# Nearest-neighbour upsampling on one core: loads in four DMAs with 32 KiB descriptors, and one broadcast copy per engine and store

## The chip, the cores and the metric

The kernel runs on one core of one Trainium2 chip. In the profiles DVE is the core's VectorE, ACT its ScalarE and SP its SyncE. The metric is the device time of one execution in microseconds; lower is better. Times quoted are medians of several executions.

## The reference

```python
x = np.random.randn(16, 64, 64, 64).astype(np.float32)      # scale_factor = 2
result = np.zeros((16, 64, 128, 128), dtype=np.float32)
for i in range(128):
    for j in range(128):
        result[:, :, i, j] = x[:, :, i // 2, j // 2]
```

Each input row of 64 floats becomes two identical output rows of 128 floats, each input element twice in a row. 16.78 MB are read and 67.11 MB are written. There is no arithmetic.

## The kernel before

The input is seen as 65536 rows of 64 floats. A tile has 128 partitions with 32 rows each: 8 KiB in, 32 KiB out, per partition. All DMAs are issued by the SyncE engine (SP in the profile) on its one queue: nine loads first (two of 1 MiB, then seven of 2 MiB), then sixteen stores of 4 MiB.

```python
K = 32                                   # input rows per partition and tile
rows = P * K                             # 4096;  16 tiles
J = 2                                    # tiles per load
... # group = 8: the whole input fits in SBUF, so one pass
k_dve = (K + 1) // 2                     # 16 rows for DVE, 16 for ACT
xpool: bufs=group;   upool: bufs=2
for ti in range(ti0, ti0 + group):       # all loads
    xt = xpool.tile([P, J, K, W], fdt, name="xt")
    ... # the first load as two DMAs of 1 MiB, the others:
    src = src.rearrange("(j p k) w -> p j (k w)", j=J, p=P)
    nc.sync.dma_start(out=xt[:, :, :, :], in_=src)
for t in range(...):                     # expand and store, tile by tile
    u2 = upool.tile([P, K, s, W, s], fdt, name="u2")
    for ei, (lo, hi) in enumerate(((0, k_dve), (k_dve, K))):
        src_ap = xt[:, j, lo:hi, :]
        for hd in range(s):
            for wd in range(s):          # four strided copies per engine
                dst = u2[:, lo:hi, hd, :, wd]
                ... # nc.vector.tensor_copy (ei == 0) or nc.scalar.copy
    nc.sync.dma_start(out=of[r0 : r0 + rows, :], in_=u2[:, :, :, :, :])
```

## Time and profile before

The kernel took 200.79 us (200.72 to 201.0, three runs). The profiled execution has a span of 199.2 us.

The next fence is the profile page of the kernel before. Part 1 gives the busy time of each engine and its share of the span. The row "DMA" is the mean busy share of the 16 DMA engines in 40 equal slices of the span, in tenths, so that 9 means full; below it stand the GB/s moved. The queue lines give packets, MB and the share of 16 engines' time. The lines with a source line give one group of instructions: output and input shape, count, then busy us and mean ns of one, then the idle time before them and what ended it.

```profile
DVE 40.0 (20%) x64; ACT 68.0 (34%) x65; POOL 0.2 (0%) x4
...
DMA  6999999999999999999999999999999999999995
...
q1 hardware_dynamic: 4496, 83.89, 98.5%
q14 instruction: 3, 0.02, 0.0%
...
DMA 69%; ACT 18%; SPq 3%; ACTq 1%; issue 0%
...
L88 ACT COPY u<-xt 128x1024 f32<-128x1024 f32 x64 | 66.7, 1136 | 114.6 <-DMA out_dram<-u 111.0
L86 DVE COPY u<-xt 128x1024 f32<-128x1024 f32 x64 | 40.0, 690 | 141.7 <-DMA out_dram<-u 136.1
```

The DMA engines are full from the second slice to the last but one. No compute engine is near full.

The share of 18% for ACT in the chain of waits needs the timeline to be read. This is two rounds of the steady state, kernel before (start us, duration us, engine, instruction; in brackets the idle time before and its releaser):

```profile
62.25 4.17 ACT L88 COPY u<-xt 128x1024 f32<-128x1024 f32 x4 [5.43 <-DMA out_dram<-u]
62.27 2.50 DVE L86 COPY u<-xt 128x1024 f32<-128x1024 f32 x4 [7.08 <-DMA out_dram<-u]
...
71.96 4.18 ACT L88 COPY u<-xt 128x1024 f32<-128x1024 f32 x4 [5.55 <-DMA out_dram<-u]
```

A store lands about every 9.7 us and frees one of two buffers. ACT refills it in 4.17 us, while the other buffer's store is on the DMA engines. The chain alternates between ACT and a store, because each is released by the other, but the DMA row stays at 9: the 4.17 us cost nothing as long as they stay below 9.7.

The trace also has a record of every DMA packet. Times in the rest of this document that are "after the first packet" count from the start of the first data packet, about 1.7 us after the start of the span. In the kernel before:

| packets | number | duration | per DMA engine |
|---|---|---|---|
| loads, 8 KiB | 2048 | median 311 ns, the first 1.1 us | 40.58 us |
| stores, 32 KiB | 2048 | 1213 ns, hardly any spread | 155.34 us |

Together 195.9 us out of the span's 199.2 us are packet time on every engine. There is no more than about 3 us that is not transfer. (The records do not name the engine of a packet; "per engine" is the sum over all packets divided by 16.)

### The profile page before, as it was taken

Reading aid. Unit: us, or ns where it says so; the run is one execution under the profiler, and the core shown is the slowest. Engines: PE = TensorE matmul, PEld = TensorE weight load, DVE = VectorE, ACT = ScalarE, POOL = GpSimd, SP = SyncE. Lnnn points to the kernel's source line nnn. Section 1 sums busy time; section 2 is a strip of 40 time slices with the busy share of each in tenths; the row PEclk is TensorE's granted clock in tenths of the full one; section 3 lists DMA queues with packets and bytes.
Section 4 is the critical chain, followed back from the end, with each engine's and each line's share of the span. In section 5 each row is a group of like instructions: output and inputs, shape, how many; then the busy total and the mean of one; then the engine's idle time right before and its main releaser. Section 6 shows DMA issues by size and latency. Waiting matters only on the chain.

```text
span 199.2 us, 246 instructions
## 1 busy us (share of the span) xinstructions
DVE 40.0 (20%) x64; ACT 68.0 (34%) x65; POOL 0.2 (0%) x4
## 2 busy tenths in 40 slices
DVE  0810000000404050505050505050505050504000
ACT  2870000000444352626161708080808080808000
POOL 0000000000000000000000000000000000000000
DMA  6999999999999999999999999999999999999995
GB/s 214 423 438 421 423 421 424 421 500 421 421 421 421 421 421 441 480 447 421 421 421 421 421 421 461 474 428 428 421 421 421 424 421 467 461 421 421 428 428 217
DMA packets 4499, 83.90 MB, mean 421 GB/s; under 512 B 401, under 2 KB 401, under 8 KB 401
## 3 DMA queue, kind: packets, MB, share of 16 engines
q1 hardware_dynamic: 4496, 83.89, 98.5%
q14 instruction: 3, 0.02, 0.0%
HBM read 16.78 MB, written 67.11 MB: 421 GB/s over the span
## 4 chain that ended last, share of the span: by engine, by line
DMA 69%; ACT 18%; SPq 3%; ACTq 1%; issue 0%
DMA out_dram<-u 67%; ACT u L88 18%; SPq L90 3%; DMA xt<-in_x_dram 2%; ACTq L121 1%; ACTq L88 0%
## 5 line engine op out<-in xcount | busy, mean ns | idle before, releaser
L88 ACT COPY u<-xt 128x1024 f32<-128x1024 f32 x64 | 66.7, 1136 | 114.6 <-DMA out_dram<-u 111.0
L86 DVE COPY u<-xt 128x1024 f32<-128x1024 f32 x64 | 40.0, 690 | 141.7 <-DMA out_dram<-u 136.1
L88 ACT ACT_TABLE_LOAD x1 | 1.3, 1283 | 0.7 <-PEq L107 0.7
L107 POOL MEMSET const-uint8-127<- 128x1 uint8 x1 | 0.1, 102 | 0.0
L107 POOL MEMSET const-bfloat16-1.0<- 128x1 bf16 x1 | 0.1, 101 | 0.0
L107 POOL MEMSET const-float32-0.0<- 128x1 f32 x1 | 0.1, 99 | 0.2 <-issue 0.2
L107 POOL MEMSET const-float32-1.0<- 128x1 f32 x1 | 0.1, 98 | 0.0
## 6 DMA issues: line engine op xcount, KB each, us to landing
out_dram<-u SPq DMA_DIRECT2D x16, 4096.0 KB, 15.1
xt<-in_x_dram SPq DMA_DIRECT2D x7, 2048.0 KB, 24.4
xt<-in_x_dram SPq DMA_DIRECT2D x2, 1024.0 KB, 5.8
```

The source lines that it names most:

```text
L86: nc.vector.tensor_copy(out=dst, in_=src_ap)
L88: nc.scalar.copy(out=dst, in_=src_ap)
L90: nc.sync.dma_start(out=of[r0 : r0 + rows, :], in_=u2[:, :, :, :, :])
L107: nc = _bacc.Bacc("TRN2", target_bir_lowering=False, num_devices=1)
L121: with _tile.TileContext(nc) as tc:
```

## The change

The change has two parts. The loads become four DMAs of 4 MiB in which a partition's share is one contiguous run of 32 KiB, and the stores, which keep their 32 KiB per partition, go to places 128 KiB apart. And the eight strided copies of a store become two: each engine writes its share of all four copies in one instruction, reading a source that is broadcast with stride 0. Of a store's 32 rows DVE now takes 18 and ACT 14, instead of 16 each. The intent is fewer and larger descriptors (each contiguous run of a partition shows as one packet in the trace: 4 x 128 load packets) and fewer instructions. The bytes, the queue and the order of DMAs stay.

```diff
-    u2_bytes = K * s * W * s * esz * 2        # (tile sizes and grouping, cut)
...
+    K, J = 32, 4
+    NB = R // (P * J * K)
+    xf = x.rearrange("b c h w -> (b c h) w").rearrange("(n p r) w -> n p r w", n=NB, p=P)
+    of = out.rearrange("b c (h hd) w -> (b c h) (hd w)", hd=s).rearrange("(n p r) w -> n p r w", n=NB, p=P)
+    KV = 18
...
-                    nc.sync.dma_start(out=xt[:, :, :, :], in_=src)
+        xt = xpool.tile([P, J * K, W], fdt, name="xt")
+        nc.sync.dma_start(out=xt[:, :, :], in_=xf[n])
...
-                    for hd in range(s):
-                        for wd in range(s):
-                            dst = u2[:, lo:hi, hd, :, wd]
-                            if ei == 0:
-                                nc.vector.tensor_copy(out=dst, in_=src_ap)
-                            else:
-                                nc.scalar.copy(out=dst, in_=src_ap)
-                nc.sync.dma_start(out=of[r0 : r0 + rows, :], in_=u2[:, :, :, :, :])
+    def expanded(rows):
+        k = rows.shape[1]
+        return rows.unsqueeze(2).unsqueeze(4).to_broadcast([P, k, s, W, s])
+            nc.vector.tensor_copy(out=u[:, :KV], in_=expanded(xts[n][:, r0 : r0 + KV, :]))
+            nc.scalar.copy(out=u[:, KV:], in_=expanded(xts[n][:, r0 + KV : r0 + K, :]))
+            nc.sync.dma_start(out=of[n, :, r0 : r0 + K, :], in_=u[:, :, :, :, :])
```

More of the change, by code (lines that the diff above doesn't have):

```diff
@@ L14 @@
     x: bass.AP,
-    scale_factor: bass.AP,
+    scale_factor: int,
     out: bass.AP,
@@ L19 @@
     P = nc.NUM_PARTITIONS
-    s = int(scale_factor) if not isinstance(scale_factor, bass.AP) else None
-    assert s is not None and s >= 1
+    s = int(scale_factor)
     B, C, H, W = x.shape
@@ L26 @@
     fdt = x.dtype
-    esz = 4 if fdt == mybir.dt.float32 else mybir.dt.size(fdt)
-    xf = x.rearrange("b c h w -> (b c h) w")
-    of = out.rearrange("b c (h hd) w -> (b c h) (hd w)", hd=s)
-    K = 32
-    while K > 1 and R % (P * K) != 0:
-        K //= 2
-    assert R % (P * K) == 0, f"{R} input rows not tileable into {P} partitions"
-    rows = P * K
-    ntiles = R // rows
-    J = 2
-    while ntiles % J != 0:
-        J //= 2
-    n_in = ntiles // J
-    u2_bytes = K * s * W * s * esz * 2
@@ L44 @@
-    xt_bytes = J * K * W * esz
-    group = max(1, min(n_in, (200 * 1024 - u2_bytes) // xt_bytes))
-    while n_in % group != 0:
-        group -= 1
-    k_dve = (K + 1) // 2
-    with (
-        tc.tile_pool(name="xin", bufs=group) as xpool,
-        tc.tile_pool(name="uexp", bufs=2) as upool,
-    ):
-        for ti0 in range(0, n_in, group):
-            xts = {}
-            for ti in range(ti0, ti0 + group):
-                xt = xpool.tile([P, J, K, W], fdt, name="xt")
-                if ti == 0:
-                    for j in range(J):
-                        nc.sync.dma_start(
-                            out=xt[:, j, :, :],
-                            in_=xf[(ti * J + j) * rows : (ti * J + j + 1) * rows, :],
-                        )
-                else:
-                    src = xf[ti * J * rows : (ti + 1) * J * rows, :]
-                    if J > 1:
-                        src = src.rearrange("(j p k) w -> p j (k w)", j=J, p=P)
-                    nc.sync.dma_start(out=xt[:, :, :, :], in_=src)
-                xts[ti] = xt
-            for t in range(ti0 * J, (ti0 + group) * J):
-                ti, j = divmod(t, J)
-                r0 = t * rows
-                xt = xts[ti]
-                u2 = upool.tile([P, K, s, W, s], fdt, name="u2")
-                for ei, (lo, hi) in enumerate(((0, k_dve), (k_dve, K))):
-                    if lo >= hi:
-                        continue
-                    src_ap = xt[:, j, lo:hi, :]
-                    for hd in range(s):
-                        for wd in range(s):
-                            dst = u2[:, lo:hi, hd, :, wd]
-                            if ei == 0:
-                                nc.vector.tensor_copy(out=dst, in_=src_ap)
-                            else:
-                                nc.scalar.copy(out=dst, in_=src_ap)
-                nc.sync.dma_start(out=of[r0 : r0 + rows, :], in_=u2[:, :, :, :, :])
@@ new lines @@
+    K, J = 32, 4
+    NB = R // (P * J * K)
+    assert NB * P * J * K == R
+    xf = x.rearrange("b c h w -> (b c h) w").rearrange(
+        "(n p r) w -> n p r w", n=NB, p=P
+    )
+    of = out.rearrange("b c (h hd) w -> (b c h) (hd w)", hd=s).rearrange(
+        "(n p r) w -> n p r w", n=NB, p=P
+    )
+    KV = 18
+    xpool = ctx.enter_context(tc.tile_pool(name="xin", bufs=NB))
+    upool = ctx.enter_context(tc.tile_pool(name="uexp", bufs=2))
+    xts = []
+    for n in range(NB):
+        xt = xpool.tile([P, J * K, W], fdt, name="xt")
+        nc.sync.dma_start(out=xt[:, :, :], in_=xf[n])
+        xts.append(xt)
@@ new lines, in expanded @@
+    def expanded(rows):
+        k = rows.shape[1]
+        return rows.unsqueeze(2).unsqueeze(4).to_broadcast([P, k, s, W, s])
+    for n in range(NB):
+        for j in range(J):
+            r0 = j * K
+            u = upool.tile([P, K, s, W, s], fdt, name="u")
+            nc.vector.tensor_copy(
+                out=u[:, :KV], in_=expanded(xts[n][:, r0 : r0 + KV, :])
+            )
+            nc.scalar.copy(
+                out=u[:, KV:], in_=expanded(xts[n][:, r0 + KV : r0 + K, :])
+            )
+            nc.sync.dma_start(
+                out=of[n, :, r0 : r0 + K, :], in_=u[:, :, :, :, :]
+            )
```

## The prediction

> **What bounds the kernel now.** The core's 16 DMA engines. The page's DMA row shows them full in 38 of 40 slices, and the queue table gives queue 1 98.5% of 16 engines' span for 83.89 MB (16.78 MB read, 67.11 MB written). ACT is 34% busy, DVE 20%. The chain of waits (DMA 69%, ACT 18%) overstates ACT: in order of time it shows ACT's 4.2 us expansion right after a store has landed, while the *other* buffer's store (15.1 us from issue to landing, a landing about every 9.7 us) is still moving. The DMA row stays at 9 throughout, so ACT is hidden.
>
> The trace's single packet records give the sum. Loads: 2048 packets of 8 KiB, median 311 ns, mean 317 ns, the first ones about 1.1 us each. Stores: 2048 packets of 32 KiB, 1213 ns nearly without spread. Per engine 128 x 0.317 = 40.6 us of loads and 128 x 1.2136 = 155.3 us of stores, 195.9 of the span's 199.2 us; 3.3 us is start and end.
>
> **What the change does.**
>
> - *Stores*: same bytes and 32 KiB packets, so I leave 155.3 us. Their rows now lie 128 KiB apart in HBM, not 32 KiB. The Trainium skill, "DMA: Bandwidth & Descriptors", section "Latency and other measured facts", reports 207 GB/s at a 512 KiB pitch against 214 at full rate; 128 KiB should be harmless. No run here shows it yet.
> - *Loads*: 512 packets of 32 KiB instead of 2048 of 8 KiB. From 309 and 1213 ns, the commonest durations, a packet costs about 8 ns plus bytes at 27.2 B/ns. The same page ("Why small descriptors are slow") gives a fixed overhead per packet; the trace agrees, but at 8 KiB it is only 2.5%. If a 32 KiB read costs 1213 ns like a write, an engine's loads take 32 x 1.213 = 38.8 us plus about 0.9 us for the slow first packet, 39.7 us: about 1 us saved, the only gain on the critical path.
> - *Compute*: 64 instructions per engine become 16. ACT per tile: before 4 x 1.136 = 4.5 us; after, 3584 elements, estimated 3.2 to 3.8 us. DVE per tile: before 4 x 0.69 us; after, 4608 elements, 2.5 us if the broadcast source keeps its rate, about 5 us if it loses a factor of two. All are under 9.7 us; none of it counts.
> - *First tile*: waits for 4 MiB, not 1 MiB: first copies at about 12 us instead of 5.56. The first store queues behind all loads (until about 42 us) anyway: nothing lost.
> - *Queue*: still SyncE alone, in the same order; fewer issues, which were hidden.
>
> **Sum.** 200.8 - 1.0 = 199.8 us. Predicted 199.8 us, 80% range 199.0 to 201.0. Chances: faster by over 2% 0.02, within 2% 0.94, slower by over 2% 0.04.
>
> **What would show it.** DMA row again 9 in all inner slices; queue 1 with about 2880 packets and some 98.5%; load packets at 1213 ns (if longer, the gain goes); store packets still 1213 ns (longer: the pitch costs); ACT about 3.5 us and DVE 2.5 to 5 us per instruction, both idle mostly for stores; DVE's first copy near 12 us; the load phase about 1 us shorter.
>
> **What would make it wrong.** Slower: the wider store pitch slows HBM writes, or a copy takes over 9 us because of its broadcast source, and then the DMA row shows gaps. Faster by over 2% would need 4 us, more than the 3.3 us outside transfers and the 1 us of load overhead leave room for in practice.

## The result

The kernel after took 200.64 us (200.58 to 200.67, four runs) against 200.89 us for the kernel before (200.72 to 201.04, four runs). The ratio is 0.999, 95% interval 0.9976 to 1.0004. The change is thus within 2%, and its gain is about 0.25 us, a quarter of the 1.0 us predicted. The interval includes no gain at all, although the four times of the one kernel do not overlap those of the other. The question is where the rest went.

The page of the kernel after, the lines that answer to those above:

```profile
DVE 40.9 (21%) x16; ACT 52.0 (26%) x17; POOL 0.2 (0%) x4
...
DMA  6999999999999999999999999999999999999994
...
q1 hardware_dynamic: 2880, 83.89, 98.5%
...
DMA 76%; ACT 14%; issue 0%; ACTq 0%
...
L59 ACT COPY u<-xt 128x3584 f32<-128x3584 f32 x16 | 50.8, 3179 | 128.9 <-DMA out_dram<-u 117.9
L56 DVE COPY u<-xt 128x4608 f32<-128x4608 f32 x16 | 40.9, 2559 | 140.2 <-DMA out_dram<-u 127.2
```

Queue 1 has 2880 packets, as predicted, and the same share. The copies are as foreseen: 2.56 us on DVE and 3.18 us on ACT per store. The line of queue 14 is gone.

The steady state of the kernel after, the same stretch of the timeline:

```profile
62.36 3.18 ACT L59 COPY u<-xt 128x3584 f32<-128x3584 f32 x1 [6.46 <-DMA out_dram<-u]
62.38 2.56 DVE L56 COPY u<-xt 128x4608 f32<-128x4608 f32 x1 [7.08 <-DMA out_dram<-u]
...
72.03 3.18 ACT L59 COPY u<-xt 128x3584 f32<-128x3584 f32 x1 [6.49 <-DMA out_dram<-u]
```

The stores still land every 9.67 us. ACT is done a microsecond earlier and waits a microsecond longer.

So the answer must be in the packet records. Here they are for both kernels; "excess" is the time of the packets above their steady durations of 309 ns (8 KiB) and 1213 ns (32 KiB), summed and divided by 16 engines. (The excess of other sizes below is counted from their medians, 611 ns for 16 KiB and 2420 ns for 64 KiB.)

| per engine, us | before | after |
|---|---|---|
| load packets, total | 40.58 | 40.47 |
| of it steady (128 x 0.309; 32 x 1.213) | 39.55 | 38.82 |
| excess of loads in the first 2.5 us | 0.57 | 0.72 |
| excess of loads from there to 36 us | 0.37 | 0.00 |
| excess of loads from 36 us on | 0.08 | 0.93 |
| loads end after the first packet | 40.62 | 40.80 |
| store packets, total | 155.34 | 155.27 |
| last store packet ends after the first packet | 196.22 | 195.69 |

Two things stand out.

The first is the seam between loads and stores. The larger packets did save what was predicted up to 36 us: 0.73 us of steady time and 0.37 us of creep (the 8 KiB packets lengthen from 309 to about 314 ns from some 13 us on). Then the last two load packets of each engine take up to 2.0 us where all before them took 1213 ns. These are the last 32 of the 512 load packets, in order of their start (ns after the first packet, ns of duration); the first store packets, from 40325 on, take 1213 ns again:

```
load packets 470 to 479:  (35972, 1213) (36008, 1213) ... (36329, 1213)
load packets 480 to 495:  (36929, 1988) (36965, 1789) (36989, 1906) (37056, 1551) ... (37539, 1280)
load packets 496 to 511:  (38528, 1794) (38538, 1921) (38633, 1848) (38655, 1812) ... (39133, 1622)
store packets from 512:   (40325, 1213) (40461, 1213) (40469, 1213) ...
```

That gives back 0.93 us, and the loads end 0.18 us later than before.

A sum of durations flatters the larger packets a little, because successive records of one engine overlap by 3 to 4 ns: in steady state packets of 8 KiB start 306 ns apart and those of 32 KiB 1209 ns apart (medians). By the starts the steady saving is 128 x 306 - 32 x 1209 ns, about 0.5 us, and not 0.73.

The second is the end. In the kernel before, two 8 KiB instruction packets run 153.05 and 153.13 us after the first packet, 309 ns each, and the store packets behind them take 1571 and 1645 ns in place of 1213. That delays two engines by 0.67 and 0.74 us (309 plus the excess), and in the end the last three engines finish at 195.85, 196.07 and 196.22 us, while the other thirteen are done by 195.51. Joining each packet to the one that starts where it ends shows that the two delayed engines are the ones that finish at 196.07 and 196.22 us; without the delay they would have finished by about 195.5, and the last end would be 195.85, some 0.4 us earlier. The kernel after has no such packet during its run, and all sixteen engines finish between 195.22 and 195.69.

The chains of waits agree. These are three successive stores in the chain of the kernel before (start us, duration us from issue to landing), and after the dots the same three of the kernel after. The store that runs during the fetch, about 154.8 us after the start of the span, takes 0.4 us longer than its neighbours in the first and not in the second. (All three are about 1 us longer in the kernel after because ACT has them ready a microsecond earlier, while stores land at the same pace.)

```profile
124.69 15.14 DMA out_dram<-u
...
144.15 15.56 DMA out_dram<-u
...
164.01 15.02 DMA out_dram<-u
...
123.66 16.05 DMA out_dram<-u
...
143.01 16.05 DMA out_dram<-u
...
162.37 16.05 DMA out_dram<-u
```

So the theory is: the gain of the loads was given back at the seam (theory S), and the gain that was measured comes from the missing instruction fetch (theory F), that is from the copies and not from the DMAs.

### The profile page after: what moved, and what is told of

It is laid out like the page before. It is cut to its first block, busy times and chain, and to the rows that moved or that the text cites. A ratio compares the mean times of both kernels' runs of the same rounds, so it can differ in the third digit from the quotient of the medians.

```text
span 198.8 us, 145 instructions
## 1 busy us (share of the span) xinstructions
DVE 40.9 (21%) x16; ACT 52.0 (26%) x17; POOL 0.2 (0%) x4
## 2 busy tenths in 40 slices
DMA packets 2880, 83.89 MB, mean 422 GB/s; under 512 B 320, under 2 KB 320, under 8 KB 320
## 3 DMA queue, kind: packets, MB, share of 16 engines
q1 hardware_dynamic: 2880, 83.89, 98.5%
## 4 chain that ended last, share of the span: by engine, by line
DMA 76%; ACT 14%; issue 0%; ACTq 0%
DMA out_dram<-u 70%; ACT u L59 14%; DMA xt<-in_x_dram 6%; ACTq L59 0%
## 5 line engine op out<-in xcount | busy, mean ns | idle before, releaser
L59 ACT COPY u<-xt 128x3584 f32<-128x3584 f32 x16 | 50.8, 3179 | 128.9 <-DMA out_dram<-u 117.9
L56 DVE COPY u<-xt 128x4608 f32<-128x4608 f32 x16 | 40.9, 2559 | 140.2 <-DMA out_dram<-u 127.2
```

What stands on the lines that cost most here:

```text
L56: nc.vector.tensor_copy(out=u[:, :KV], in_=expanded(xts[n][:, r0 : r0 + KV, :]))
L59: nc.scalar.copy(out=u[:, KV:], in_=expanded(xts[n][:, r0 + KV : r0 + K, :]))
```

## The experiments

Fourteen kernels were run.

### Copies alone and DMAs alone

e1 is the kernel before with only the copies replaced:

```diff
-  # four tensor_copy and four scalar.copy into u2[:, lo:hi, hd, :, wd]
+  nc.vector.tensor_copy(out=u2[:, :KV], in_=expanded(xt[:, j, :KV, :]))
+  nc.scalar.copy(out=u2[:, KV:], in_=expanded(xt[:, j, KV:K, :]))
```

> The kernel before with only the copies replaced (one per engine and store, broadcast source); all DMAs as before. Theory F (instruction fetch): in the kernel before two 8 KiB instruction packets about 153 us after the first data packet delay two DMA engines by about 0.7 us, and these two end last; with a quarter of the copy instructions the fetch is gone, so the engines' last end falls from 196.2 to about 195.5 us after the first packet and the time by 0.3 to 0.6 us, to about 200.4. Rival D (the small gain comes from the larger load packets): DMAs are unchanged, so the time stays at 200.8 to 200.9.

e2 is the kernel after with the eight strided copies of the kernel before:

```diff
-  nc.vector.tensor_copy(out=u[:, :KV], in_=expanded(...))
-  nc.scalar.copy(out=u[:, KV:], in_=expanded(...))
+  for hd in range(s):
+      for wd in range(s):
+          nc.vector.tensor_copy(out=u[:, :16, hd, :, wd], in_=xts[n][:, r0 : r0 + 16, :])
+          nc.scalar.copy(out=u[:, 16:, hd, :, wd], in_=xts[n][:, r0 + 16 : r0 + K, :])
```

> The kernel after with the old copies (four strided copies per engine and store). Theory F: the instruction fetch in mid-run is back, the time is no better than before, 200.8 to 201.2, and the last two load packets of each engine are still stretched to 1.5 to 1.9 us. Rival D: the gain stays, 200.6.

Measured: e1 200.49 us (200.38 to 200.70) and e2 200.93 us (200.83 to 201.11), with the kernel before at 200.92 us. The ratios are 0.9981 (0.9968 to 0.9994) and 1.0003 (0.9990 to 1.0015). The page of e1, queues:

```profile
q1 hardware_dynamic: 4496, 83.89, 98.7%
```

And the page of e2, queues:

```profile
q1 hardware_dynamic: 2880, 83.89, 98.4%
q14 instruction: 2, 0.02, 0.0%
```

In e1 the instruction packets are gone and the last engine ends at 195.78 us, although its 8 KiB load packets lost 0.22 us at the seam in this execution (0.06 to 0.10 in the other kernels with 8 KiB loads). In e2 they are back, at 152.91 and 152.96 us, and the last engine ends at 195.98 us. The new copies alone give the small gain, 0.43 us; the new DMAs alone give nothing. This is what theory F expects and not what its rival does. That it comes from the copies being fewer instructions rather than faster ones is shown by e12 below, where few instructions take longer per store (4.43 us) than ACT's four did in the kernel before (4.17 us), no instruction packet appears, and the time stays at that of the kernel after. No run adds a fetch alone. The Trainium skill, "Runtime: NRT & Kernel Launch", section "Instruction fetch mechanics", says that instructions are fetched in blocks of 16 KiB by a DMA queue that the sequencer drives, and that the cost is "mostly hidden". Two packets of 8 KiB add up to such a block. The trace agrees with the size of the block; no run here shows what drives the fetch. Here the cost was not hidden: it fell on DMA engines that were full, and two of them ended last.

### Packet size or store pitch?

The seam could come from the larger load packets (S) or from the stores' new places (P). e3 is the kernel after with each load cut into four DMAs of 8 KiB per partition, so that only the stores' pitch is new:

```diff
-        nc.sync.dma_start(out=xt[:, :, :], in_=xf[n])
+        for j in range(J):
+            nc.sync.dma_start(out=xt[:, j * K : (j + 1) * K, :], in_=xf[n, :, j * K : (j + 1) * K, :])
```

> The kernel after with each load cut into four DMAs of 8 KiB packets; the stores keep their 128 KiB pitch. Theory S (the seam belongs to large load packets): no load packet at the end of the loads is stretched beyond about 0.42 us, the load phase is about 40.6 us as before, time 200.4 to 200.6. Rival P (the seam belongs to the 128 KiB store pitch): about 0.9 us per engine is still lost between the last loads and the first stores, time about 201.4.

e4 is the kernel after with the stores at the old pitch. Its result is wrong, since the rows then land in wrong places:

```diff
+    of2 = out...rearrange("(n j p r) w -> n j p r w", n=NB, j=J, p=P)
-                out=of[n, :, r0 : r0 + K, :], in_=u[:, :, :, :, :]
+                out=of2[n, j], in_=u[:, :, :, :, :]
```

> The kernel after with the stores put where the kernel before put its own, 32 KiB pitch; the result is wrong on purpose. Theory S: the last two 32 KiB load packets of each engine are stretched as in the kernel after, about 0.9 us per engine, time 200.6. Rival P: the stretch is gone, the load phase is 39.8 us, time 199.7.

Measured: e3 200.34 us (ratio 0.9970, 0.9957 to 0.9984), e4 200.66 us (0.9990, 0.9978 to 1.0003). In e3 the excess from 36 us on is 0.10 us and the loads end at 40.54 us; in e4 it is 0.87 us and they end at 40.83 us. The store packets take 1213 ns at both pitches. The rival P falls: the pitch costs nothing that shows, and the loss at the seam goes with the load packets. In e3 one load packet at the seam takes 531 ns; no other is above the 420 ns expected.

### How much with other sizes?

e5 cuts only the last of the four loads into 8 KiB packets, e7 cuts every load into two DMAs of 16 KiB per partition, and e14 makes two loads of 64 KiB per partition.

```diff
 e5:  if n < NB - 1: nc.sync.dma_start(out=xt[:, :, :], in_=xf[n])
      else: # four DMAs as in e3
 e7:  for j in range(2): nc.sync.dma_start(out=xt[:, j*2*K : (j+1)*2*K, :], in_=xf[n, :, j*2*K : (j+1)*2*K, :])
 e14: -    K, J = 32, 4
      +    K, J = 32, 8
```

> The kernel after with only the last of the four loads cut into four DMAs of 8 KiB packets. Theory S (what is stretched are 32 KiB load packets that run just ahead of queued stores): the first three loads keep 32 KiB packets of 1213 ns, the last packets are near 309 ns, so both losses are avoided: load phase 40.0 to 40.2 us, time 199.7 to 200.1. Rival E (the loss goes with the change-over from large load packets to anything, or with the loads as a whole): about 0.9 us is lost at the change from 32 to 8 KiB packets or at the end of the loads, time 200.5 to 200.7.

> The kernel after with each load cut into two DMAs of 16 KiB packets. If the loss at the seam grows with the size of the load packets: about 0.3 to 0.5 us per engine at the seam, load phase 40.2 us, time about 200.2. If any packet above 8 KiB has it in full: 0.9 us at the seam, time 200.6. If only 32 KiB has it: none, time about 199.9.

> The kernel after with two loads of 8 MiB and 64 KiB a partition. If the transfer stays one packet of 64 KiB (about 2420 ns) and the loss at the seam grows with the packet size, it is over 1 us per engine and the time is 200.7 to 201.2. If the seam loss is bounded, about 0.9 us, the time is 200.5 to 200.7. If the row is cut into smaller packets, the record sizes show it and the result is that of the smaller size.

Measured, with the kernel after for comparison:

| kernel | load packets | time, us | ratio (95%) | excess from 36 us, us per engine |
|---|---|---|---|---|
| e3 | 8 KiB | 200.34 | 0.9970 (0.9957 to 0.9984) | 0.10 |
| e7 | 16 KiB | 200.31 | 0.9972 (0.9960 to 0.9985) | 0.68 |
| after | 32 KiB | 200.64 | 0.9990 (0.9976 to 1.0004) | 0.93 |
| e14 | 64 KiB | 200.58 (one run) | | 1.09 |
| e5 | 32 KiB, last load 8 KiB | 200.41 | 0.9980 (0.9968 to 0.9993) | 0.52 |

The loss grows with the packet size, with a falling slope. e5 is a miss: it was to combine the gain of both and reach 199.7 to 200.1 us, but half a microsecond is lost at the seam although its last packets are of 8 KiB. The loss is therefore not simply that of the size of the last packets; it may also depend on how fast the loads before went, which no run tests by itself. Across the sizes the packet time of all loads comes out nearly the same, 40.5 us per engine with 8, 16, 32 and 64 KiB (40.53, 40.50, 40.47 and 40.50). e7's expectation was met in its time (200.2 expected) but not in its parts, since the loads end at 40.80 us as in the kernel after. e14 met the one branch of its expectation in its seam (over 1 us) and the other in its time (200.58 us), so its loss at the seam did not show in its one time.

### Are the queued stores needed?

e6 expands the blocks from the last to the first, so that no store can be issued before the last load has landed:

```diff
-    for n in range(NB):
+    for n in (3, 2, 1, 0):
         for j in range(J):
```

> The kernel after with the blocks expanded in the order 3, 2, 1, 0, so that no store is issued before all loads have landed. If queued stores stretch the last loads (theory S), then the last two load packets of each engine take 1213 ns, the load phase ends at about 39.9 us after the first packet, and a hole of some 5 us follows (ACT 3.2 us, plus landing and issue): about 204.5 to 206. If the last load packets are long by themselves (rival: the end of the last load's memory or of the ring), they are still at 1.5 to 1.9 us here.

It took 205.24 us (one run). The DMA rows of its page:

```profile
DMA  7999999909999999999999999999999999999995
GB/s 264 451 419 412 419 464 451 419 0 412 451 477 412 412 412 412 509 419 412 412 412 425 502 412 412 412 412 502 425 412 412 412 432 496 412 412 412 412 502 219
```

The zero in the ninth slice is the hole made on purpose. Before it, every load packet after the first ones takes 1213 ns, the last two included; the excess from 36 us on is 0.00, and the loads end 39.91 us after the first packet. The loads have then really landed: the first copy starts at 42.11 us of the span, 0.4 us after the loads' last packet ends, and in the kernel after the first copy (13.01 us of the span) also starts 0.4 us after the first load's last packet (10.92 us after the first packet). So the end of the loads by itself stretches nothing. Without stores behind them the 32 KiB load packets do bring their gain.

To have the same for 8 KiB packets, e9 was e3 with the order of blocks of e6:

> The kernel after with 8 KiB load packets and the blocks expanded in the order 3, 2, 1, 0, so that no store is queued behind the loads. It tells what 8 KiB load packets cost by themselves, beside the 32 KiB packets under the same order, whose loads ended 39.92 us after the first packet. If the larger packets do save about 1 us of load time (0.74 us of fixed cost per packet plus the creep from 309 to 314 ns), the loads end here at 40.5 to 41.0 us and the time is about 206.0. If the creep and the loss at the seam both come from the queued stores and the packet size saves only its fixed cost, the packets stay at 309 ns and the loads end at about 40.4. If the size saves nothing, they end at 39.9.

It took 200.41 us (one run), with no hole. The experiment failed to make its condition: the last block is loaded by four DMAs, and its first piece needs only the first of these, so that a store was issued before the loads ended. e13 takes the pieces in the order 3, 2, 1, 0 as well:

> As e9, but the pieces within a block are also taken in the order 3, 2, 1, 0, so that the first store needs the very last load and nothing is queued behind the loads. With 32 KiB packets and nothing queued (e6) the loads ended 39.92 us after the first packet. If 8 KiB packets cost 1 us more by themselves (their fixed cost and the creep to 314 ns), they end at 40.4 to 40.9 us here and the creep is there without stores. If the creep is due to queued stores, the packets stay at 309 ns and the loads end at about 40.2 to 40.4 us. If packet size costs nothing, they end at 39.9. Time 205.5 to 206.5, for the hole after the loads.

It took 205.66 us (one run), and the loads end at 40.54 us. The creep is there without any store queued. The four cases side by side:

| load packets, us per engine (loads end) | stores queued behind | none queued |
|---|---|---|
| 8 KiB | 40.53 (40.54), e3 | 40.42 (40.54), e13 |
| 32 KiB | 40.47 (40.80), after | 39.40 (39.91), e6 |

Without stores behind them the larger packets save 40.42 - 39.40 = 1.02 us of packet time and 0.62 us of the end of the loads. With stores behind them they save 0.06 us of packet time, and the end is 0.26 us later. Measured from each engine's first start to its last end, where overlapping records do not count twice, the loads take on average 40.1 us in e13 and 39.3 in e6, about 0.8 us less, but 40.2 in e3 and 40.4 in the kernel after, 0.2 us more. In e6 and e13 alike the stores after the hole took 156.10 us of packet time per engine, 0.83 more than in the kernel after; why is not shown, but being the same in both it does not touch this comparison of the loads.

e10 asks whether the stores must have waited long. The blocks are expanded in the order 2, 3, 0, 1, so that the first store is issued only a few microseconds before the seam:

> The kernel after with the blocks expanded in the order 2, 3, 0, 1: the first store is issued about 34 us after the first packet instead of 14, still some 3 us before the last two load packets of each engine start. If a store queued behind is enough (theory S), the stretch is the same, 0.9 us per engine, and the time is 200.5 to 200.8. If the loss needs stores that have waited long, it shrinks and the time falls to about 199.8.

200.59 us (one run), 0.95 us of excess from 36 us on. A store queued shortly before is enough.

e8 asks whether the stores' own packet size matters, and cuts the first store into four DMAs of 8 KiB packets:

```diff
+            q = K // 4 if (n, j) == (0, 0) else K
+            for c in range(0, K, q):
+                nc.sync.dma_start(out=of[n, :, r0 + c : r0 + c + q, :], in_=u[:, c : c + q])
```

> The kernel after with the first store alone cut into four DMAs of 8 KiB packets. If the stretch of the last loads comes from 32 KiB packets of the first store being read while the last loads are still being written, the stretch shrinks to below 0.4 us per engine and the time falls to about 200.1. If only the size of the load packets matters, 0.9 us remains and the time is about 200.6 to 200.8.

200.68 us (ratio 0.9992, 0.9977 to 1.0007), 0.92 us of excess. It does not matter.

### Is the copying hidden?

e12 gives the whole expansion to DVE:

```diff
-            nc.vector.tensor_copy(out=u[:, :KV], ...);  nc.scalar.copy(out=u[:, KV:], ...)
+            nc.vector.tensor_copy(out=u[:, :], in_=expanded(xts[n][:, r0 : r0 + K, :]))
```

> The kernel after with the whole expansion on DVE, nothing on ACT: 8192 elements in about 4.5 us per store instead of 2.56 on DVE and 3.18 on ACT. If all of the copying is hidden behind the 9.7 us in which a store occupies the DMA engines, the time is unchanged, 200.5 to 200.8. If the 14% of the chain of waits that stand against ACT were real, adding 1.3 us to each of 14 waits would add up to 18 us.

200.63 us (ratio 0.9986, 0.9971 to 1.0001), as the kernel after. From its page:

```profile
DMA  7999999999999999999999999999999999999995
...
DMA 71%; DVE 20%; issue 0%; DVEq 0%
...
L56 DVE COPY u<-xt 128x8192 f32<-128x8192 f32 x16 | 70.7, 4427 | 112.2 <-DMA out_dram<-u 99.2
```

The copy of a store takes 4.43 us instead of 3.18, the share of the chain rises from 14 to 20%, and the time does not move. ACT can be left idle. This is the cleanest proof that the compute engines' part of the chain costs nothing in the kernel after; for the kernel before it is inferred, since its 4.17 us per store lie below the 4.43 us tried here.

### The stores on another queue

The change keeps all DMAs on the SyncE queue. e11 issues the stores from ACT instead:

```diff
-            nc.sync.dma_start(
+            nc.scalar.dma_start(
                 out=of[n, :, r0 : r0 + K, :], in_=u[:, :, :, :, :]
```

> The kernel after with the stores issued by ACT on its own queue, so that loads and stores mix on the DMA engines from the time the first store is issued. Bytes and engines are the same; if the engines' time per packet is what counts, 200.3 to 201.0. If each change from load to store on an engine costs what the one seam costs (about 0.9 us), dozens of changes would make it over 205. If loads and stores overlap when mixed, it is below 199.

Measured: 210.71 us, ratio 1.0492 (1.0474 to 1.0509). By its number this is the second expectation (over 205), but not for the reason given there. The DMA row of its page, and two rounds of its timeline (ACTq is a DMA issue by ACT's sequencer):

```profile
DMA  8999999999999997999799979997999799989996
```

```profile
72.43 3.18 ACT L59 COPY u<-xt 128x3584 f32<-128x3584 f32 x1 [9.66 <-DMA out_dram<-u]
...
82.06 3.18 ACT L59 COPY u<-xt 128x3584 f32<-128x3584 f32 x1 [6.45 <-DMA out_dram<-u]
82.12 3.49 ACTq L62 DMA_DIRECT2D out_dram<-u  x2
```

The DMA row has a 7 in every fourth slice from the sixteenth on (the last time an 8). The first tile's copy is done at 75.61 us, but its store is issued at 82.12 us, after ACT has passed the next copy, which waits for a buffer until 82.06. The source has copies and stores by turns, but by these times ACT goes through them in pairs: two copies, then two stores. On a queue shared with the copies a store that is ready thus waits behind a copy that is not. The packets took 196.4 us per engine, 0.7 more than in the kernel after, while the span grew by 9.8 us (198.8 to 208.6), so mixing loads and stores is not what cost the 10 us; the holes are.

## Why the prediction was wrong in its size

- *The bound was right.* The DMA engines are full in both kernels, and e12 shows that the ACT and DVE part of the chain is hidden in the kernel after.
- *Stores were right.* Store packets of 1213 ns at a pitch of 128 KiB, as at 32 KiB (e4). The page cited in the prediction has no figure for this pitch, so it is the step from 512 down to 128 KiB that the trace bears out.
- *Copies were right in duration.* DVE 2.56 us, so the broadcast source kept its rate, and ACT 3.18 us, at the lower edge of the range given (3.2 to 3.8). The first copy came at 13.0 us, a microsecond later than predicted, without effect.
- *The step that failed is the term for the loads*: "39.7 us: about 1 us saved, the only gain on the critical path". Measured, the load packets took 40.47 us per engine against 40.58, so 0.1 us was saved, and the loads ended 0.18 us later than before. The saving itself exists: e6 against e13 shows 1.02 us of packet time, or about 0.8 us from first start to last end. It was given back at the change from loads to stores, where the last two 32 KiB packets of each engine took up to 2.0 us. The prediction took the steady duration of a packet for all packets but the first, and did not ask what happens at the last (its own list of signs had it: "if longer, the gain goes"). Nothing in the trace of before showed it, because its 8 KiB packets lose only 0.08 us there.
- *A term was missing.* "The only gain on the critical path" was wrong the other way too: the copies, priced at nothing, brought 0.43 us (e1) by sparing an instruction fetch on full DMA engines. The line of queue 14 on the page of before could have shown it. With both corrections the sum is about -0.43 from the copies and +0.01 from the DMAs (e2); the change measured -0.25 us, within the intervals of about 0.26 us on these differences. That the time fell at all, as predicted, was luck: it did not come from the loads.

What stays open is why a queued store stretches the load packets ahead of it. Shown is that it needs stores queued behind (e6), that a few microseconds in the queue are enough (e10), that it grows with the load packets (e3, e7, e14), and that neither the stores' pitch (e4) nor their packet size (e8) matters. That the load packets' total comes to 40.5 us whatever their size suggests one common limit for loads that stores follow, but no run shows what that limit is. Open too is whether e3 and e7 are really faster than the kernel after: their medians are about 0.3 us lower, but the intervals overlap, and in the profiled executions their last packets end at 195.66 and 195.69 us, as in the kernel after (195.69).

No version beats both kernels by an amount that matters. The best were e7 (200.31 us) and e3 (200.34 us), 0.3% below the kernel before.

## What to carry to other kernels

When the DMA engines are full to the last slices, price a change in packet time per engine and look at the packets at the seams (first, last, change of direction), since a gain in the steady packets can be lost there. A compute engine's share in the chain of waits is no cost while the DMA row stays full; but a larger program can cost DMA time through its instruction fetch, so read the small queues of the page as well. Keep stores off a queue whose engine also does copies that wait for buffers, or check the order in which that engine's program issues them.

## What the Trainium skill lacked or had wrong

- "DMA: Bandwidth & Descriptors", "Why small descriptors are slow (HBM only)": a fixed cost per packet is there, and the trace agrees that there is one (about 8 ns by the durations of 309 and 1213 ns, about 5 ns by the starts, 306 and 1209 ns apart). Missing is that load packets ahead of queued stores are stretched, the more the larger they are: 0.10, 0.68, 0.93 and 1.09 us per engine with 8, 16, 32 and 64 KiB, and 0.00 us with 32 KiB and no store queued. Larger load descriptors brought nothing here.
- The same page, same place: 8 KiB load packets crept from 309 to about 314 ns from 13 us on, 0.3 to 0.4 us in all, with or without stores queued; 32 KiB load packets did not. No page has it.
- "Runtime: NRT & Kernel Launch", "Instruction fetch mechanics": calls the cost of a block boundary "mostly hidden". With DMA engines 98.5% busy one block (two packets of 8 KiB) delayed two engines by 0.67 and 0.74 us, and these ended last; sparing it with the DMAs unchanged (e1) was worth 0.43 us.
- "DMA: Bandwidth & Descriptors", "Rules for kernel authors": says that spreading DMAs over issuing engines does not help bandwidth and only saves issue time. It does not warn that it can cost: stores issued from ACT, behind copies that wait for buffers, took 10 us more (210.71 us).
